# A hybrid decoder step on one core: the feed-forward's down projection as seven block products instead of eight, for 18 of its 22 feature tiles

## The chip, the cores and the metric

The kernel runs on one core of a Trainium2 chip. TensorE (PE) multiplies matrices into PSUM, VectorE (DVE), ScalarE (ACT) and GpSimd (POOL) work on tiles of 128 partitions, and SyncE (SP) and ACT issue transfers between DRAM and on-chip memory. The engines run side by side and wait for each other by semaphores. The metric is the device time of one execution in microseconds.

## The reference, cut to what matters

One layer of a decoder trunk for 1024 prompt tokens and 8 x 4 sample tokens (1056 columns in all): a mixer block, cross-attention, a feed-forward block and the final norm. The change touches the feed-forward block alone:

```python
u = rmsnorm(h, W['norm_ffn'][l])
h = h + (jax.nn.silu(u @ W['w_ffn_gate'][l]) * (u @ W['w_ffn_up'][l])) @ W['w_ffn_down'][l]
...
y = rmsnorm(h, W['norm_final'])
```

The model width is 1024 (8 tiles of 128), the hidden width 2816 (22 feature tiles of 128). All values are float32.

## The kernel before

*Precision.* Every large product is made of three matmuls: an operand is split into a rounded part (hi, by ACT) and the rest (lo, by DVE or POOL), and hi x hi, lo x hi and hi x lo are summed in PSUM.

*Layout.* Features lie on the partitions and the 1056 tokens along the free axis. For block products the tokens are halved (`TH` = 528 columns), and each half is cut in two again for PE (`HB` = 264 columns, index c).

*Gate and up.* The loop `for f in range(NF2)` takes feature tiles two at a time (11 pairs f), first a gate phase, then an up phase. Each phase multiplies a 2 x 2 block of weights by a 2 x 2 block of activations with seven block products instead of eight (`PRODUCTS`, `strassen`). The right-hand blocks (B11, B21, B22 and the sums T1 to T4 of the activations) are made once, ahead of the loop, in `sides`, and stay in 28 slots of the pool `sl`. The left-hand blocks are made on the way by `lefts`: for each pair of weight tiles POOL makes two sums (s1, s3), DVE two (s2, s4), then ACT and DVE split the seven blocks; `ahead_of` keeps that work two weight pairs ahead.

The block products land in PSUM tiles `st` (three buffers for four sums G[0] to G[3]). After product i the callback `gate` or `up` moves sums out of PSUM. Its first step (i = 0) is a copy of G[0] by ACT; the third product (i = 2) adds into the same G[0], so PE may begin it only after the copy. In the gate phase the results get SiLU; in the up phase they are multiplied into the four quarters s11, s12, s21, s22 of the pair's gated result (two by POOL, two by DVE; s12 comes last). Then four transfers on ACT's queue store the quarters in `hid_dram`. The quarters live in a ring of five tiles (`slot2`, `temps`).

*Down.* After the loop the 22 hidden tiles are read back (`load_hidden`), split, and multiplied by the down weights in four groups of 6, 6, 6 and 4 tiles (`FGROUPS`): for each of the 8 output tiles, and for three chunks of 352 columns, PE makes 6 x 3 matmuls (`unit`, L151 to L153), and DVE adds the PSUM tile to the residual h (L1414), which was kept in `h_dram`. In the fourth group the output is finished in three stretches of columns (`LAST`): sum, squares for the final norm, scaling, store.

*Order.* The instructions of PE and SP stand in the order of the code; those of ACT, DVE and POOL are put in order by a scheduler when the kernel is built. Every engine works through its own row of instructions.

Of the kernel before, what the change touches and what calls it, by code (L numbers as in the profile page):

```python
# [15 lines left out]
P = 128  # L16
# [4 lines left out]
NCH = 3  # L21
# [4 lines left out]
FT = FF // P  # L26
FGROUPS = ((0, 6), (6, 6), (12, 6), (18, 4))
LAST = ((0, 384), (384, 768), (768, T))
# [29 lines left out]
def hybrid_step(ctx, tc, xT, memT, consts_d, masks_d, wbd_d, poolw_d, spool_d, w_kv, w_xbc, w_dt, w_lg, w_pool, w_z, h0_d,  # L58
# [173 lines left out]
    h_dram = dr.tile([P, 8, T], F32, name="h_dram")  # L232
    hid_dram = dr.tile([P, FT, T], F32, name="hid_dram")

# [1001 lines left out]
    def lefts(pairs):  # L1236

        raws = []

        def load(i):  # L1240
            r = [fp.tile([P, DM], F32, tag="ar", name=nm("ar"), bufs=4, padded_shape=[P, T]) for _ in range(2)]
            for k in range(2):
                for t, src in zip(r, pairs[i]):
                    nc.sync.dma_start(t[:, k * 512:k * 512 + 512], src[:, k * 512:k * 512 + 512])
            raws.append(r)

        load(0)
        for i in range(len(pairs)):
            (a11, a12), (a21, a22) = [(t[:, :512], t[:, 512:]) for t in raws.pop(0)]
# [3 lines left out]
            s1, s2, s3, s4 = sa[:, :512], sa[:, 512:], sb[:, :512], sb[:, 512:]  # L1253
            nc.gpsimd.tensor_tensor(s1, a21, a22, op=OP.add)
            nc.gpsimd.tensor_tensor(s3, a11, a21, op=OP.subtract)
            nc.vector.tensor_tensor(s2, s1, a11, op=OP.subtract)
            nc.vector.tensor_tensor(s4, a12, s2, op=OP.subtract)
            for n, srcs in enumerate(((a11, s2), (a12, s3), (s1, a22), (s4,))):
                pool, b = (fp, "b") if n % 2 else (wp, "")
                hi, lo = (pool.tile([P, DM], F32R, tag=b + t, name=nm(t), bufs=2) for t in ("whi", "wlo"))  # L1260
                for j, src in enumerate(srcs):
                    a = slice(j * 512, j * 512 + 512)
                    nc.scalar.activation(hi[:, a], src, AF.Copy)  # L1263
                    nc.vector.tensor_tensor(lo[:, a], src, hi[:, a].bitcast(F32), op=OP.subtract)  # L1264
                yield [(hi[:, j * 512:j * 512 + 512], lo[:, j * 512:j * 512 + 512]) for j in range(len(srcs))]

# [13 lines left out]
    NF2 = FT // 2  # L1280
    blocks = ahead_of(lefts([(w_gu[j, 2 * f], w_gu[j, 2 * f + 1]) for f in range(NF2) for j in range(2)]))

    def product(i, w, G, c, kk):
        xb, g, begins = PRODUCTS[i]
        whi, wlo = w
        for k in range(kk):
            a, b = k * P, k * P + P
            xh, xl = X[xb, k, c]
            out = G[g][:, c, :HB]
# [4 lines left out]

    def strassen(kk, after, by_part):

# [12 lines left out]
        for i in range(7):  # L1309
            g = PRODUCTS[i][1]  # L1310
            if g not in G:
                G[g] = ps.tile([P, 2, 512], F32, tag="st", name=nm("st"), bufs=3)
            w = next(blocks)
            for c in range(2):
                product(i, w, G, c, kk)
            after(i, slice(0, 2), G)

    def temps():
        t = slot2(F32, "tm")
        return [t[:, i * TH:(i + 1) * TH].rearrange("p (c t) -> p c t", c=2) for i in range(2)]  # L1320

    add, sub, mul = OP.add, OP.subtract, OP.mult
    for f in range(NF2):
# [28 lines left out]
        v22, v12 = temps()  # L1352
        v21, _ = temps()

        def up(i, cs, G):
# [17 lines left out]
            else:  # L1373
                vec(u2, u2, at(2), op=add)
                vec(s12[:, cs], s12[:, cs], u2, op=mul)

        strassen(4, up, f == NF2 - 1)
        for n, t in enumerate(ga):
            nc.scalar.dma_start(hid_dram[:, 2 * f + n // 2, n % 2 * TH:(n % 2 + 1) * TH], t.rearrange("p c t -> p (c t)"))
    drain()  # L1380
    fp_.close()
# [6 lines left out]
    with tc.tile_pool(name="fq", bufs=1, reuse_waits="tile") as fp:  # L1388
        hids = []

        def load_hidden():
            f = len(hids)
            hi, lo = slot(F32R, "hh"), slot(F32R, "hl")
            nc.sync.dma_start(lo.bitcast(F32), hid_dram[:, f, :])
            nc.scalar.activation(hi, lo.bitcast(F32), AF.Copy)
            nc.vector.tensor_tensor(lo, lo.bitcast(F32), hi.bitcast(F32), op=OP.subtract)
            hids.append((hi, lo))

        weights = one_ahead([(w_down[m, :, f0 * P:(f0 + nf) * P], nf * P) for f0, nf in FGROUPS[:-1] for m in range(8)])
        for _ in range(FGROUPS[0][1]):  # L1400
            load_hidden()
        h = [slot2(F32, "h") if m < 5 else slot(name="h") for m in range(8)]
        nc.sync.dma_start(h[0], h_dram[:, 0, :])
        for f0, nf in FGROUPS[:-1]:
            for m in range(8):
                w = next(weights)
                if f0 == 0 and m < 7:
                    nc.sync.dma_start(h[m + 1], h_dram[:, m + 1, :])
                if len(hids) < min(f0 + nf + 6, FT):
                    load_hidden()  # L1410
                for c in range(NCH):
                    p = mmps()
                    unit(p, w, hids[f0:f0 + nf], ch(c), nf)
                    nc.vector.tensor_tensor(h[m][:, ch(c)], h[m][:, ch(c)], p, op=OP.add)  # L1414
        f0, nf = FGROUPS[-1]
        hid = hids[f0:]
        ws = []

        def last_strip():
            t = slot(F32R, "wd")  # L1420
            m = len(ws)
            split_into(w_down[m, :, f0 * P:(f0 + nf) * P], nf * P, t[:, :nf * P], t[:, nf * P:2 * nf * P])
            ws.append((t[:, :nf * P], t[:, nf * P:2 * nf * P]))

        while len(ws) < 8:
            last_strip()

        def finish(a, b, sq, n0, n1):
# [25 lines left out]
        for a, b in LAST:  # L1454
            for m in range(8):
                p = ps.tile([P, b - a], F32, tag="mm", name=nm("mm"), bufs=3)
                unit(p, ws[m], hid, slice(a, b), nf)
                hc = h[m][:, a:b]
                nc.vector.tensor_tensor(hc, hc, p, op=OP.add)
                sq = fp.tile([P, b - a], F32, tag="sq", name=nm("sq"), bufs=3, padded_shape=[P, 384])  # L1460
                if m:
# [6 lines left out]
            spawn(finish(a, b, sq, *((3, 3) if b < T else (0, 0))))  # L1468
        drain()
    ps_.close()  # L1470

# [4 lines left out]
def _layout(i):  # L1476
# [66 lines left out]
    a["w_gu"] = np.stack([strips(i["w_ffn_gate"][0]), strips(i["w_ffn_up"][0])])  # L1543
    a["w_down"] = strips(i["w_ffn_down"][0])
    return a
# [36 lines left out]
```

## Time and profile before

| | |
|---|---|
| time, median of 3 runs | 1827.39 us (1826.93 to 1829.48) |
| profiled execution | 1827.24 us, span 1825.3 us, mean granted clock 0.986 |
| gate and up phases | from 1073.5 us to 1546.2 us of the span |
| a pair f (gate and up) in steady state | 41.0 us |
| down, first 18 feature tiles | to 1760.5 us |
| down, last 4 tiles, and final norm | to 1825.3 us |

The page of the profile gives busy times; "granted clock" is the share of full speed that PE's clock had. A row of a timeline has start, duration, engine, line of the code, operation, and what it writes and reads (by the program's names, with shapes), and in brackets how long the engine stood idle before it and what ended that. "ACTq" is a transfer issued by ACT. In `st<-x,whi`, st is a PSUM tile, x a right-hand block and whi a left-hand block.

### The profile page before, as it was taken

Reading aid. Unit: us, or ns where it says so; the run is one execution under the profiler, and the core shown is the slowest. Engines: PE = TensorE matmul, PEld = TensorE weight load, DVE = VectorE, ACT = ScalarE, POOL = GpSimd, SP = SyncE. Lnnn points to the kernel's source line nnn. Section 1 sums busy time; section 2 is a strip of 40 time slices with the busy share of each in tenths; the row PEclk is TensorE's granted clock in tenths of the full one; section 3 lists DMA queues with packets and bytes.
Section 4 is the critical chain, followed back from the end, with each engine's and each line's share of the span. In section 5 each row is a group of like instructions: output and inputs, shape, how many; then the busy total and the mean of one; then the engine's idle time right before and its main releaser. Section 6 shows DMA issues by size and latency. Waiting matters only on the chain.

```text
span 1825.3 us, 30861 instructions
## 1 busy us (share of the span) xinstructions
PE 1747.0 (96%) x12043; PEld 1694.2 (93%) x12043; DVE 1091.0 (60%) x2043; ACT 743.5 (41%) x1445; POOL 533.2 (29%) x584
## 2 busy tenths in 40 slices
PE   8899999999999999999999879999999999999997
PEld 7798888888999999999999768999999999999997
DVE  5888997798744434455565587555555555443335
ACT  6544443577634213355564453322322223211134
POOL 2423557664342222212220332222222221000014
PEclk9999999999999999999999978999999999999999
DMA  9111123341322512144352132222222223532212
GB/s 347 56 61 61 62 63 90 103 143 56 128 82 74 191 60 94 66 144 128 116 181 96 34 129 87 78 71 76 86 72 77 77 73 132 195 98 93 80 50 96
DMA packets 96130, 182.84 MB, mean 100 GB/s; under 512 B 14192, under 2 KB 29168, under 8 KB 95984
## 3 DMA queue, kind: packets, MB, share of 16 engines
q1 hardware_dynamic: 78128, 147.04, 24.6%
q10 hardware_dynamic: 17856, 33.83, 5.0%
q8 instruction: 94, 1.54, 0.3%
q14 instruction: 52, 0.43, 0.1%
HBM read 144.24 MB, written 36.59 MB: 99 GB/s over the span
## 4 chain that ended last, share of the span: by engine, by line
PE 79%; DVE 10%; issue 3%; POOL 3%; ACT 2%; DMA 2%; SPq 0%; ACTq 0%; DVEq 0%; POOLq 0%
PE mm L151 15%; PE mm L153 15%; PE mm L152 15%; PE st L1291 8%; PE st L1292 8%; PE st L1290 8%; DVE cy L502 2%; PE poa L1081 1%; PE pss L1063 1%; DVE x L329 1%; POOL seg L574 1%; PE poz L1012 1%; DVE x L1179 1%; PE psa L1012 1%; DVE seg L557 1%
## 5 line engine op out<-in xcount | busy, mean ns | idle before, releaser
L1290 PE MATMUL st<-x,whi 128*128 128x264 f32 x1232 | 353.3, 287 | 7.7 <-DVE tm L1341 6.1
L1291 PE MATMUL st<-x,whi 128*128 128x264 f32 x1232 | 352.7, 286 | 3.1 <-DVE x L1179 3.1
L1292 PE MATMUL st<-x,wlo 128*128 128x264 f32 x1232 | 353.0, 287 | 0.5 <-DVE wlo L1264 0.5
L151 PE MATMUL mm<-uh,whi 128*128 128x352 f32 x960 | 319.9, 333 | 0.0
L153 PE MATMUL mm<-uh,wlo 128*128 128x352 f32 x960 | 310.5, 323 | 0.0
L152 PE MATMUL mm<-ul,whi 128*128 128x352 f32 x960 | 310.2, 323 | 0.0
L1290 PEld LDWEIGHTS st<-x,whi 128*128 128x128 f32 x1232 | 234.3, 190 | 8.8 <-DVE tm L1341 6.3
L1291 PEld LDWEIGHTS st<-x,whi 128*128 128x128 f32 x1232 | 233.8, 190 | 3.6 <-DVE x L1179 3.6
L1292 PEld LDWEIGHTS st<-x,wlo 128*128 128x128 f32 x1232 | 234.2, 190 | 0.9 <-DVE wlo L1264 0.9
L151 PEld LDWEIGHTS mm<-uh,whi 128*128 128x128 f32 x960 | 181.1, 189 | 4.3 <-issue 1.9
L152 PEld LDWEIGHTS mm<-ul,whi 128*128 128x128 f32 x960 | 181.6, 189 | 2.5
L153 PEld LDWEIGHTS mm<-uh,wlo 128*128 128x128 f32 x960 | 181.0, 189 | 0.0
L121 ACT ACTIVATE whi<-wraw 128x512 fp32r<-128x512 f32 (+1 forms) x176 | 100.3, 596 | 176.1 <-PE mm L152 143.6
L151 PE MATMUL mm<-hh,whi 128*128 128x352 f32 x432 | 140.3, 325 | 3.0 <-ACT whi L121 3.0
L153 PE MATMUL mm<-hh,wlo 128*128 128x352 f32 x432 | 140.2, 324 | 0.8 <-DVE wlo L122 0.8
L152 PE MATMUL mm<-hl,whi 128*128 128x352 f32 x432 | 139.9, 324 | 0.0
L122 DVE TENSOR_TENSOR wlo<-wraw,whi 128x512 fp32r<-128x512 f32 (+1 forms) x144 | 100.2, 721 | 23.3 <-ACT whi L121 22.9
L1414 DVE TENSOR_TENSOR h<-h,mm 128x352 f32<-128x352 f32 x72 | 37.4, 520 | 106.4 <-PE mm L153 106.4
L1263 ACT ACTIVATE whi<-as 128x512 fp32r<-128x512 f32 x88 | 54.8, 624 | 93.5 <-PE st L1291 74.6
L956 POOL TENSOR_TENSOR kvlo<-kvraw,kvhi 128x512 fp32r<-128x512 f32 x32 | 41.4, 1295 | 162.6 <-ACT kvhi L955 124.4
L1464 POOL TENSOR_TENSOR acc_mem<-acc_mem,sq 128x384 f32<-128x384 f32 (+1 forms) x18 | 17.6, 978 | 240.7 <-ACT sq L1462 240.2
L151 PEld LDWEIGHTS mm<-hh,whi 128*128 128x128 f32 x432 | 81.6, 189 | 3.3 <-ACT whi L121 3.3
(444 smaller groups left out, 4097.4 us busy)
## 6 DMA issues: line engine op xcount, KB each, us to landing
ar<-w_gu SPq DMA_DIRECT2D x88, 256.0 KB, 3.7
hid_dram<-tm ACTq DMA_DIRECT2D x44, 264.0 KB, 2.1
hl<-hid_dram SPq DMA_DIRECT2D x22, 528.0 KB, 4.1
h_dram<-h ACTq DMA_DIRECT2D x16, 528.0 KB, 2.9
h<-h_dram SPq DMA_DIRECT2D x16, 528.0 KB, 5.2
seg<-acs_dram SPq DMA_DIRECT2D x32, 256.0 KB, 3.6
wraw<-w_out SPq DMA_DIRECT2D x32, 256.0 KB, 3.6
kvraw<-kc_d SPq DMA_DIRECT2D x32, 256.0 KB, 2.9
```

The lines of the kernel that those rows point to most:

```text
L121: nc.scalar.activation(hi[:, a:b], raw, AF.Copy)
L122: (second if a else nc.vector).tensor_tensor(lo[:, a:b], raw, hi[:, a:b].bitcast(F32), op=OP.subtract)
L151: nc.tensor.matmul(out, whi[:, a:b], xh[:, cols], start=k == 0, stop=False)
L152: nc.tensor.matmul(out, whi[:, a:b], xl[:, cols], start=False, stop=False)
L153: nc.tensor.matmul(out, wlo[:, a:b], xh[:, cols], start=False, stop=k == kk - 1)
L502: nc.vector.scalar_tensor_tensor(y[:, :n], raw[:, j:j + n], w[j], y[:, :n], op0=OP.mult, op1=OP.add)
L956: eng.tensor_tensor(lo, src, hi.bitcast(F32), op=OP.subtract)
L1263: nc.scalar.activation(hi[:, a], src, AF.Copy)
L1290: nc.tensor.matmul(out, whi[:, a:b], xh, start=begins and k == 0, stop=False, skip_group_check=True)
L1291: nc.tensor.matmul(out, whi[:, a:b], xl, start=False, stop=False, skip_group_check=True)
L1292: nc.tensor.matmul(out, wlo[:, a:b], xh, start=False, stop=k == kk - 1, skip_group_check=True)
L1414: nc.vector.tensor_tensor(h[m][:, ch(c)], h[m][:, ch(c)], p, op=OP.add)
```

## The change

The down products of the first 18 feature tiles (9 pairs) become seven block products as well, in three groups of three pairs; the last four tiles stay as they were.

- The right-hand blocks are now quarters of the gated result and four sums of them. At the end of each of the first nine pairs f, POOL makes T1 to T4 from the quarters, and ACT's queue stores seven tiles of 528 columns (s11, s21, s22, T1 to T4) in place of four.
- `load_right` reads such a block back, ACT rounds it, and DVE (every third time POOL) makes the rest. Each group needs 21 of them (7 products x 3 pairs), each in one of the 28 slots; `feed` loads them as slots come free, in the last up phase and in the fourth block (m = 3) of each group.
- The down weights go through `lefts` too, in pairs of output tiles (width 384 instead of 512), and `down` adds the block products into h: three additions on POOL, six operations on DVE, one copy on ACT for each pair of output tiles.
- One PSUM pool serves gate, up and down; the change to the pool of the last stage comes after the down groups. The first loads of the down stage are issued in the second half of the last up phase.

The core of the diff:

```diff
-FGROUPS = ((0, 6), (6, 6), (12, 6), (18, 4))
+NG, GK = 3, 3
+F0 = NG * GK * 2
+NB8 = ("B11", "B12", "B21", "B22", "T1", "T2", "T3", "T4")
...
-    hid_dram = dr.tile([P, FT, T], F32, name="hid_dram")
+    hid_dram = dr.tile([P, FT // 2, 8, TH], F32, name="hid_dram")
...
+    def load_right():
+        b, f = next(rights)
+        t = slot(F32R, "xd")
+        hi, lo = t[:, :TH], t[:, TH:]
+        nc.sync.dma_start(lo.bitcast(F32), hid_dram[:, f, NB8.index(b)])
+        nc.scalar.activation(hi, lo.bitcast(F32), AF.Copy)
+        (nc.gpsimd if len(hids) % 3 == 2 else nc.vector).tensor_tensor(lo, lo.bitcast(F32), hi.bitcast(F32), op=OP.subtract)
+        hids.append(t)
+        for c in range(2):
+            X[b, 4 + f, c] = hi[:, c * HB:(c + 1) * HB], lo[:, c * HB:(c + 1) * HB]
...
+            if f == NF2 - 1 and cs.start == 0 and i == 6:
+                feed(12)
+                load_h(0)
+                load_h(1)
+            elif f == NF2 - 1 and cs.start == 1:
+                feed({0: 2, 4: 4, 5: 3}.get(i, 0))
 
         strassen(4, up, f == NF2 - 1)
-        for n, t in enumerate(ga):
-            nc.scalar.dma_start(hid_dram[:, 2 * f + n // 2, n % 2 * TH:(n % 2 + 1) * TH], t.rearrange("p c t -> p (c t)"))
+        if f < NG * GK:
+            t1, t3, t2, t4 = v22, v12, v21, v11
+            for t, x, y in ((t1, s12, s11), (t2, s22, t1), (t3, s22, s12), (t4, s21, t2)):
+                nc.gpsimd.tensor_tensor(t, x, y, op=sub)
+            parts = zip((0, 2, 3, 4, 5, 6, 7), (s11, s21, s22, t1, t2, t3, t4))
+        else:
+            parts = enumerate(ga)
+        for n, t in parts:
+            nc.scalar.dma_start(hid_dram[:, f, n], t.rearrange("p c t -> p (c t)"))
...
+    for g in range(NG):
+        for m in range(4):
...
+            def down(i, cs, G):
+                at = lambda g: G[g][:, cs, :HB]
+                vec, gp = nc.vector.tensor_tensor, nc.gpsimd.tensor_tensor
+                if i == 0:
+                    nc.scalar.activation(u3, at(0), AF.Copy)
+                elif i == 1:
+                    vec(u2, u3, at(1), op=add)
+                    gp(h12, h12, u2, op=add)
+                elif i == 2:
+                    vec(h11, h11, at(0), op=add)
+                elif i == 3:
+                    vec(u3, u3, at(1), op=add)
+                    gp(h22, h22, u3, op=add)
+                    gp(h21, h21, u3, op=add)
...
+                if m == 3:
+                    feed(3)
+
+            strassen(GK, down, k0=4 + g * GK)
```

How the rows of ACT change where one pair f ends and the next begins (here the sixth and the seventh). First before: the last two of the four stores of the quarters (tm_14053 and tm_14054 hold them), weight splits (whi), then the copy of the next pair's first product (tm_14493<-st):

```order
L1379 DMA hid_dram<-tm_14054 128x528
L1263 ACTIVATE whi_14553<-as_14393 128x512
L1379 DMA hid_dram<-tm_14053 128x528
L1333 ACTIVATE tm_14493<-st_14495 128x528
L1263 ACTIVATE whi_14620<-ar_14386 128x512
```

Now, at the same place (tm_14306 and tm_14307 hold the four sums):

```order
L1446 DMA hid_dram<-tm_14089 128x528
L1266 ACTIVATE whi_14595<-as_14428 128x512
L1446 DMA hid_dram<-tm_14306 128x528 x2
L1446 DMA hid_dram<-tm_14307 128x528 x2
L1387 ACTIVATE tm_14535<-st_14537 128x528
L1266 ACTIVATE whi_14662<-ar_14421 128x512
```

One store, of a quarter, stood ahead of the copy (L1333); four, of the sums, stand ahead of it now (L1387).

POOL at the same place, before: the two gated quarters, then two sums of the weights of the next pair:

```order
L1369 TENSOR_TENSOR tm_14053<-tm_14053,tm_14271 128x528
L1372 TENSOR_TENSOR tm_14054<-tm_14054,tm_14272 128x528
L1254 TENSOR_TENSOR as_14614<-ar_14387 128x512
L1255 TENSOR_TENSOR as_14615<-ar_14386,ar_14387 128x512
L1254 TENSOR_TENSOR as_14832<-ar_14609 128x512
```

And now:

```order
L1423 TENSOR_TENSOR tm_14088<-tm_14088,tm_14306 128x528
L1426 TENSOR_TENSOR tm_14089<-tm_14089,tm_14307 128x528
L1257 TENSOR_TENSOR as_14656<-ar_14422 128x512
L1258 TENSOR_TENSOR as_14657<-ar_14421,ar_14422 128x512
L1441 TENSOR_TENSOR tm_14306<-tm_14088,tm_14089 128x528
L1441 TENSOR_TENSOR tm_14306<-tm_14088 128x528
L1441 TENSOR_TENSOR tm_14307<-tm_14088,tm_14306 128x528
L1441 TENSOR_TENSOR tm_14307<-tm_14089,tm_14307 128x528
L1257 TENSOR_TENSOR as_14874<-ar_14651 128x512
```

The four sums (L1441) stand behind the weight sums (L1257, L1258), and the second and the fourth read the one before.

ACT where the second down group ends and the third begins, a place that before had no like (xd are right-hand blocks, whi weight splits, hh the first whole hidden tile for the last stage, tm<-st the copy of the third group's first product):

```order
L1266 ACTIVATE whi_18548<-ar_18328 128x384
L1337 ACTIVATE xd_18401<-xd_18401 128x528
L1337 ACTIVATE xd_18405<-xd_18405 128x528
L1266 ACTIVATE whi_18548<-as_18542 128x384
L1337 ACTIVATE xd_18434<-xd_18434 128x528
L1353 ACTIVATE hh_18438<-hl_18439 128x1056
L1465 ACTIVATE tm_18443<-st_18444 128x528
```

The copy stands last, behind the group's right-hand blocks and the hidden tile.

More of the change, by code (lines that the diff above doesn't have):

```diff
@@ L1280, in hybrid_step, with product @@
     NF2 = FT // 2
-    blocks = ahead_of(lefts([(w_gu[j, 2 * f], w_gu[j, 2 * f + 1]) for f in range(NF2) for j in range(2)]))
-    def product(i, w, G, c, kk):
+    GW = 2 * GK * P
+    blocks = ahead_of(lefts([(w_gu[j, 2 * f], w_gu[j, 2 * f + 1], 512) for f in range(NF2) for j in range(2)] +
+                            [(w_down[2 * m, :, g * GW:(g + 1) * GW], w_down[2 * m + 1, :, g * GW:(g + 1) * GW], GK * P)
+                             for g in range(NG) for m in range(4)]))
+    def product(i, w, G, c, kk, k0=0):
         xb, g, begins = PRODUCTS[i]
@@ L1293, in product, with strassen @@
         tick()
-    def strassen(kk, after, by_part):
+    def strassen(kk, after, by_part=False, k0=0):
         G = {}
@@ L1320, in temps, with load_h, load_hidden, last_strip @@
         return [t[:, i * TH:(i + 1) * TH].rearrange("p (c t) -> p c t", c=2) for i in range(2)]
+    rights = iter([(f"{PRODUCTS[i][0]}", g * GK + k) for g in range(NG) for i in range(7) for k in range(GK)])
+    hids = []
+    def load_right():
[8 more added lines that the diff above has]
+            X[b, 4 + f, c] = hi[:, c * HB:(c + 1) * HB], lo[:, c * HB:(c + 1) * HB]
+    def load_h(m):
+        h[m] = slot(name="h") if m < 3 else slot2(F32, "h")
+        nc.sync.dma_start(h[m], h_dram[:, m, :])
+    hid, ws = [], []
+    def load_hidden():
+        f = F0 + len(hid)
+        hi, lo = slot(F32R, "hh"), slot(F32R, "hl")
+        nc.sync.dma_start(lo.bitcast(F32), hid_dram[:, f // 2, f % 2 * 2:f % 2 * 2 + 2].rearrange("p s t -> p (s t)"))
+        nc.scalar.activation(hi, lo.bitcast(F32), AF.Copy)
+        nc.vector.tensor_tensor(lo, lo.bitcast(F32), hi.bitcast(F32), op=OP.subtract)
+        hid.append((hi, lo))
+    def last_strip():
+        t = slot(F32R, "wd")
+        m, nf = len(ws), FT - F0
+        split_into(w_down[m, :, F0 * P:], nf * P, t[:, :nf * P], t[:, nf * P:2 * nf * P])
+        ws.append((t[:, :nf * P], t[:, nf * P:2 * nf * P]))
+    tail = [load_hidden] * 4 + [last_strip] * 8
+    room = [0]
+    def feed(n):
+        room[0] += n
+        while len(hids) < 7 * NG * GK and room[0] >= 1:
+            load_right()
+            room[0] -= 1
+        while len(hids) == 7 * NG * GK and tail and room[0] >= (2 if tail[0] is load_hidden else 1):
+            room[0] -= 2 if tail[0] is load_hidden else 1
+            tail.pop(0)()
     add, sub, mul = OP.add, OP.subtract, OP.mult
@@ L1380, in hybrid_step @@
+    while tail:
+        tail.pop(0)()
     drain()
-    fp_.close()
     ps_.close()
@@ L1387, in hybrid_step @@
     ps = ps_.enter_context(tc.tile_pool(name="ps3", bufs=4, space=PSUM, reuse_waits="tile"))
[L1388 to L1426, printed above, removed]
+    if True:
         def finish(a, b, sq, n0, n1):
@@ L1543, in _layout @@
     a["w_gu"] = np.stack([strips(i["w_ffn_gate"][0]), strips(i["w_ffn_up"][0])])
-    a["w_down"] = strips(i["w_ffn_down"][0])
+    at = [2 * GK * g + 2 * k + j for g in range(NG) for j in range(2) for k in range(GK)] + list(range(F0, FT))
+    a["w_down"] = c(strips(i["w_ffn_down"][0]).reshape(8, P, FT, P)[:, :, at]).reshape(8, P, FF)
     return a
```

41 lines of the change are left out of this document (29 added, 12 removed).

## The prediction

> **What bounds the kernel now.** I read the page's busy shares and its chain first, then the windows of the feed-forward stages, then the timeline at one boundary between two pairs of feature tiles.
>
> ```profile
> span 1825.3 us, 30861 instructions
> PE 1747.0 (96%) x12043; PEld 1694.2 (93%) x12043; DVE 1091.0 (60%) x2043; ACT 743.5 (41%) x1445; POOL 533.2 (29%) x584
> PE 79%; DVE 10%; issue 3%; POOL 3%; ACT 2%; DMA 2%; SPq 0%; ACTq 0%; DVEq 0%; POOLq 0%
> ```
>
> PE is nearly full, and the chain runs through it. What the change touches lies after 1073 us, so the windows there give the price of a matmul (columns: stretch, its length, then busy time and number of instructions by engine, granted clock, DMA share, GB/s):
>
> ```profile
> 1200.00:1400.00 200.00, 200.00 (x1642) 200.00 (x1641) 103.84 (x145) 56.47 (x97) 47.02 (x29) 1.00 0.24 78
> 1546.50:1560.00 13.50, 9.93 (x50) 9.64 (x51) 7.22 (x11) 4.98 (x7) 0.00 (x0) 0.87 0.83 294
> 1560.00:1612.00 52.00, 52.00 (x325) 52.00 (x324) 20.89 (x35) 10.74 (x17) 0.00 (x0) 1.00 0.43 140
> ```
>
> The block products (264 columns) come every 200/1642 = 0.1218 us, the down matmuls (352 columns) every 52/325 = 0.160 us, and in both PE waits for nothing. A whole block of the gate or up phase is 168 matmuls, 20.5 us; one of its seven products is 24, 2.92 us. So matmuls saved are time saved, and any wait put before PE is time lost. The entry to the down stage is the one place there where PE waits:
>
> ```profile
> 1545.94 0.28 PE L1292 MATMUL st<-x,wlo 128*128 128x264 f32 x1
> 1549.27 0.43 PE L151 MATMUL mm<-hh,whi 128*128 128x352 f32 x1 [3.05 <-ACT whi L121]
> 1550.66 0.50 PE L153 MATMUL mm<-hh,wlo 128*128 128x352 f32 x1 [0.80 <-DVE wlo L122]
> 1550.96 0.49 PE L151 MATMUL mm<-hh,whi 128*128 128x352 f32 x1
> L151 PE MATMUL mm<-hh,wd x96: 290/337/442, 1760.5 to 1813.0; 128*128 128x384 f32 x64, 128*128 128x288 f32 x32
> ```
>
> From 1546.06 to 1760.5 the 18 tiles take 214.4 us.
>
> **The change, part by part.**
>
> *Products.* Before: 3 groups x 8 output tiles x 3 chunks x 6 tiles x 3 matmuls = 1296, at 0.160 us 207.4 us. After: 3 groups x 4 pairs x 7 products x 2 halves x 3 tiles x 3 = 1512 narrower ones, at 0.1218 us 184.2 us. That is -23.2 us. The other 214.4 - 207.4 = 7.0 us is the old entry (its gaps, and matmuls at half rate after them); it goes: -7.0 us. What is late there next comes below.
>
> *The four sums at each pair's end.* This term decides. The end of one pair and the start of the next, before, on all engines (start, duration, engine, line):
>
> ```profile
> 1344.45 0.70 DVE L1375 TENSOR_TENSOR tm<-tm,tm 128x528 f32<-128x528 f32 x1
> 1344.67 1.63 POOL L1255 TENSOR_TENSOR as<-ar,ar 128x512 f32<-128x512 f32 x1 [2.08 <-issue]
> 1345.07 1.78 DVE L1257 TENSOR_TENSOR as<-ar,as 128x512 f32<-128x512 f32 x1
> 1345.19 0.33 ACTq L1379 DMA_DIRECT2D hid_dram<-tm  x1
> 1345.61 0.61 ACT L1333 ACTIVATE tm<-st 128x528 f32<-128x528 f32 x1 [3.63 <-DMA ar<-w_gu]
> 1346.87 0.28 PE L1292 MATMUL st<-x,wlo 128*128 128x264 f32 x1
> 1346.99 0.28 PE L1290 MATMUL st<-x,whi 128*128 128x264 f32 x1
> ```
>
> DVE finishes the last gated quarter at 1345.15. ACT issues its transfer at 1345.19, as soon as that is done, and only then (1345.61) runs the copy of the next pair's first product out of PSUM, though that product ended near 1344.3. ACT works in order: the copy waits behind a transfer that waits. The copy ends at 1346.22; at 1346.99 PE begins the third product (24 matmuls after 1344.07), which adds into the bank just copied. So PE has 0.77 us to spare.
>
> Changed, the copy stands behind four more transfers, one for each sum, and POOL makes the sums after the quarter and after its row of L1255 (same work, ends 1346.30). Their price is from POOL's own 528-wide products of two tiles (a group's mean in 1300 to 1500 us; then one overlapped with DVE):
>
> ```profile
> L1369 POOL TENSOR_TENSOR tm<-tm,tm 128x528 f32<-128x528 f32 x4 | 5.3, 1323 | 45.9 <-DVE tm L1368 45.9
> L1372 POOL TENSOR_TENSOR tm<-tm,tm 128x528 f32<-128x528 f32 x4 | 6.8, 1705 | 6.4 <-DVE tm L1371 6.4
> 1339.63 1.81 DVE L1264 TENSOR_TENSOR wlo<-ar,whi 128x512 fp32r<-128x512 f32 x1
> 1339.19 1.70 POOL L1372 TENSOR_TENSOR tm<-tm,tm 128x528 f32<-128x528 f32 x1 [1.61 <-DVE tm L1371]
> ```
>
> Two-input work of DVE and POOL at once stretches both: 1.70 us on POOL for 1.32, 1.81 on DVE for 0.68. The first sum meets the rest of DVE's L1257, so 1.70; behind that DVE waits for ACT's copy, so the other three take 1.32: the last ends at 1351.97. Issue and gap as before (1345.61 - 1345.19 = 0.42) and the copy (0.61) bring 1353.0. PE waits 1353.0 - 1346.99 = 6.0 us. After a wait of that length the clock is slow:
>
> ```profile
> 1093.63 0.59 PE L1290 MATMUL st<-x,whi 128*128 128x264 f32 x1 [6.07 <-DVE tm L1341]
> 1094.02 0.42 PE L1291 MATMUL st<-x,whi 128*128 128x264 f32 x1
> 1094.24 0.42 PE L1292 MATMUL st<-x,wlo 128*128 128x264 f32 x1
> 1096.88 0.30 PE L1292 MATMUL st<-x,wlo 128*128 128x264 f32 x1
> 1097.03 0.28 PE L1290 MATMUL st<-x,whi 128*128 128x264 f32 x1
> ```
>
> Fifteen matmuls from 1093.63 took 3.40 us in place of 15 x 0.1218 = 1.83: 1.6 us more. So 7.6 us at each of the nine pairs that make sums: +68 us. Behind the waiting transfers on ACT are the copy, whose readers are DVE's first sum of products and PE, and two weight splits; those have a lead of five products and cost nothing. Bounds: four sums at 1.32 us and a full clock 5.6 x 9 = 50; four at 1.70 with the slow clock 8.7 x 9 = 78. I take 68, as both its rows are of this form and length.
>
> *Three more stores a pair* (264 KB) are nine times 0.8 MB where the DMA share is 0.24 (first window); hidden, and with no other cover needed.
>
> *The down stage's new waits.* Each group needs 21 right-hand blocks of half a hidden tile, loaded only as the group before frees its slots in its fourth block. A block is now 126 matmuls, 15.3 us, a product 2.19 us. The nearest rows are the whole tiles, of twice the width (landing; ACT; DVE; and what the transfers reached):
>
> ```profile
> hl<-hid_dram SPq DMA_DIRECT2D x22, 528.0 KB, 4.1
> L1395 ACT ACTIVATE hh<-hl x22: 1070/1087/1089, 1530.0 to 1713.9; 128x1056 fp32r<-128x1056 f32 x22
> L1396 DVE TENSOR_TENSOR hl<-hl,hh x22: 1250/1258/1259, 1531.1 to 1715.1; 128x1056 fp32r<-128x1056 f32 x22
> 1554.00:1558.00 4.00, 4.00 (x26) 4.00 (x25) 1.28 (x2) 1.09 (x1) 0.00 (x0) 0.96 1.04 410
> ```
>
> In the next group's first block ACT's copy stands behind 18 of the 21 splits; in the third group behind all, and behind a whole hidden tile of the tail. PE wants that copy at 15.3 + 2 x 2.19 = 19.7 us after the fourth block began. The last slots are free at 13.1 us (product 6), or 15.3 for the tail's tile. With 4.1 us to land, halves of 1.09 us to split (0.54 each, three) and 0.61 for the copy this is 19.4 us for the second group; for the third, 15.3 + 4.1 + 1.09 + 0.61 = 21.1. Twenty-one blocks and a weight pair are 6.5 MB, 15.9 us at 410 GB/s, beginning at 2.2: no slack either. I take 5 us at each of the two, slow clock included. At the entry the splits begin inside the last up phase, and ACT's first copy stands behind all 21 and a weight split that waits for PE's second product: 6 us. The change of PSUM pools moves to the tail: 1 us. Together +17 us. Bounds: 0, if all lands early, and 35, if each of the three is 8.4 us behind (the second rival) and the slow clock follows each (3 x 1.6) with the rest as it is (about 5).
>
> **Sum.** The profiled execution took 1827.24 us (span 1825.3 and 1.9 around it), the median is 1827.39. 1827.24 - 23.2 - 7.0 + 68 + 17 = 1882.0; 0.15 more for the median: 1882 us, 3.0% slower.
>
> **Rivals.**
>
> *Faster: the waiting transfers don't hold ACT's copy.* If a store that waits let the copy pass, the nine stalls would vanish: 1827.4 - 30.2 + 17 = 1814 us. It decides from the last sum's transfer being issued by 1345.9 in the rows above. Against it: 1345.19 and 1345.61, and the copy's 3.63 us of idle time with its product long done. Chance 0.06.
>
> *The shared work of POOL and DVE sets the down stage.* Around a group's change 14 splits on DVE (half of 1.258, 8.8 us) and 7 on POOL (1.32, 9.2 us) are added to two blocks, each of which already has on POOL three sums at 1.32 and two 384 wide of about 1.0 (5.9 us) and on DVE nine operations 384 wide of about 0.5 us (0.68 at 512; 4.6 us). Laid end to end that is 39 us in 30.7: 8.4 us behind at each change, 25 at three, in place of 16: 1891 us, and with the slow clock after each 1896. The rows at 1339 us show the two engines stretching each other, though not fully: POOL's operation had begun first and was lengthened all the same. The Trainium skill ("SBUF — State Buffer", section "SBUF: two separate sides") calls that port pair an exclusive lock, held for a whole instruction while the other blocks. By that rule the operations do lie end to end and the time is this rival's; POOL's 1.70 for 1.32 says that the one that came first is slowed too, so the trace agrees with the sum of both more than with the lock. Chance 0.17.
>
> *The clock stays up.* Without the half-rate stretch: 9 x 6.0 = 54, 1868 us. Against it stand both gaps quoted (6.07 us, and 3.05 us followed by matmuls 0.30 us apart where 0.160 is normal). Chance 0.10.
>
> *Half hidden.* If POOL begins the sums as soon as the quarter is there (1345.2) and runs them at half the price, PE waits some 2 us and keeps its clock: 9 x 2 = 18, 1832 us. No row of POOL has such a price (0.66 us for 528). Chance 0.07.
>
> **How the numbers follow.** My forecast 0.60, the rivals 0.06, 0.17, 0.10, 0.07. The forecast's own range is 1864 (50 for 68) to 1900 (78 for 68 and 8 more in the down stage). The range asked reaches down to 1855, with the clock rival and an undisturbed down stage, and up to 1905, with the port rival and dearer sums; it leaves out the faster and the half-hidden rival and a little above. What a measurement can tell from no change is 0.2%, 3.7 us: faster 0.06, same 0.02, slower 0.92.
>
> **What the profile after would show.** At nine places 41 us and a wait apart, a PE idle of about 6 us before the third product of a gate phase, released by ACT's copy, which itself stands right behind four hid_dram stores, and a granted clock below 1 behind each; POOL rows of about 1.32 us on the sums' line, the first of each four longer. In the down stage 264-wide matmuls 0.122 us apart, and waits only in the first block of a group. The forecast is wrong if PE's rows at the third product show no idle time, or if the down stage, from the last up matmul to the first of the last four tiles, isn't near 201 us.

## The result, and the profile after

The changed kernel took 1911.8 us (median of 4 runs, 1907.1 to 1913.9) against 1828.4 us for the kernel before, run beside it (4 runs, 1826.9 to 1829.7): a ratio of 1.0453, with a 95% interval of 1.0429 to 1.0476. That is 4.5% slower. The forecast was 1882 us with a range from 1855 to 1905: the sign was right, the loss was 83 us where 55 were expected, and the time lies above the range. The profiled run took 1910.1 us, its span is 1908.3.

First the page's totals of the changed kernel (span, then busy time by engine):

```profile
span 1908.3 us, 31899 instructions
PE 1754.3 (92%) x12259; PEld 1698.2 (89%) x12259; DVE 1176.0 (62%) x2127; ACT 782.3 (41%) x1538; POOL 705.5 (37%) x701
```

PE's share fell from 96 to 92%. Where it fell is read from three rows of PE's groups: the third matmul of the gate and up products (its first and last start bound the feed-forward stage) of the kernel before,

```profile
L1292 PE MATMUL st<-x,wlo x1232: 279/285/422, 1074.0 to 1545.9; 128*128 128x264 f32 x176
```

the same of the kernel after, and its first product of the last four feature tiles, which ends the down stage:

```profile
L1298 PE MATMUL st<-x,wlo x1232: 279/285/422, 1075.0 to 1621.2; 128*128 128x264 f32 x176
L153 PE MATMUL mm<-hh,wd x96: 288/337/443, 1843.2 to 1896.3; 128*128 128x384 f32 x64, 128*128 128x288 f32 x32
```

The feed-forward stage grew from 471.9 to 546.2 us, +74.3. The down stage (1621.2 to 1843.2) takes 222.0 us, and took 214.6: +7.4, where 201 had been forecast. What follows took 65.1 us after and 64.8 before. The waits of PE in the kernel after (engine, line, releaser; total, count, longest):

```profile
PE st L1296 <- ACT tm L1387: 52.4, 9, 5.8
PE st L1296 <- DVE h L1476: 13.9, 2, 7.1
PE st L1296 <- ACT tm L1465: 12.1, 3, 6.1
```

The first row is the nine gate phases. One boundary between two pairs, all engines but PE, then PE itself:

```profile
1385.96 1.78 DVE L1260 TENSOR_TENSOR as<-ar,as 128x512 f32<-128x512 f32 x1
1387.15 1.75 POOL L1441 TENSOR_TENSOR tm<-tm,tm 128x528 f32<-128x528 f32 x1
1388.86 1.29 POOL L1441 TENSOR_TENSOR tm<-tm 128x528 f32<-128x528 f32 x1
1388.93 4.21 ACTq L1446 DMA_DIRECT2D hid_dram<-tm  x4
1390.12 2.66 POOL L1441 TENSOR_TENSOR tm<-tm,tm 128x528 f32<-128x528 f32 x2
1393.18 0.61 ACT L1387 ACTIVATE tm<-st 128x528 f32<-128x528 f32 x1 [10.31 <-POOL tm L1441]
```

```profile
1387.76 0.28 PE L1298 MATMUL st<-x,wlo 128*128 128x264 f32 x1
1393.85 0.59 PE L1296 MATMUL st<-x,whi 128*128 128x264 f32 x1 [5.80 <-ACT tm L1387]
1394.23 0.42 PE L1297 MATMUL st<-x,whi 128*128 128x264 f32 x1
...
1396.43 0.42 PE L1298 MATMUL st<-x,wlo 128*128 128x264 f32 x1
...
1396.83 0.28 PE L1297 MATMUL st<-x,whi 128*128 128x264 f32 x1
```

Read from the bottom up: PE starts its third product at 1393.85 because ACT's copy ended; the copy began at 1393.18 because the last of four stores had been issued; the stores were issued one by one as POOL's sums ended, from 1388.93 on. Then PE runs at half rate (a matmul every 0.22 us) until 1396.65.

The second row of the waits was not in the forecast. Around the first change of group, DVE and POOL stand so:

```profile
1687.14 0.69 DVE L1472 TENSOR_TENSOR tm<-tm,st 128x528 f32<-128x528 f32 x1
1687.76 0.69 DVE L1338 TENSOR_TENSOR xd<-xd 128x528 fp32r<-128x528 f32 x1
1687.91 1.70 POOL L1473 TENSOR_TENSOR h<-h,tm 128x528 f32<-128x528 f32 x1 [1.88 <-PE st L1298]
1688.38 1.65 DVE L1267 TENSOR_TENSOR wlo<-ar,whi 128x384 fp32r<-128x384 f32 x1
...
1689.58 1.61 POOL L1474 TENSOR_TENSOR h<-h,tm 128x528 f32<-128x528 f32 x1
1689.95 1.65 DVE L1267 TENSOR_TENSOR wlo<-as,whi 128x384 fp32r<-128x384 f32 x1
1691.15 3.32 POOL L1338 TENSOR_TENSOR xd<-xd 128x528 fp32r<-128x528 f32 x2
1691.52 3.51 DVE L1338 TENSOR_TENSOR xd<-xd 128x528 fp32r<-128x528 f32 x2
1694.96 0.69 DVE L1476 TENSOR_TENSOR h<-h,st 128x528 f32<-128x528 f32 x1
```

L1476 takes product 5's result out of PSUM; product 7 adds into the same bank, 2.19 us after product 5 ends. It stands in DVE's row behind two weight splits of 1.65 us and two block splits of 1.75 us each, and DVE is never idle: PE waited until 1695.71 (7.11 us). This is in the fourth block of the group, where the next group's blocks are loaded, not in the first block of the next group.

### The profile page after: what moved, and what is told of

It is laid out like the page before. It is cut to its first block, busy times and chain, and to the rows that moved or that the text cites. A ratio compares the mean times of both kernels' runs of the same rounds, so it can differ in the third digit from the quotient of the medians.

```text
span 1908.3 us, 31899 instructions
## 1 busy us (share of the span) xinstructions
PE 1754.3 (92%) x12259; PEld 1698.2 (89%) x12259; DVE 1176.0 (62%) x2127; ACT 782.3 (41%) x1538; POOL 705.5 (37%) x701
## 5 line engine op out<-in xcount | busy, mean ns | idle before, releaser
L1296 PE MATMUL st<-x,whi 128*128 128x264 f32 x1232 | 363.6, 295 | 62.7 <-ACT tm L1387 52.4
L1297 PE MATMUL st<-x,whi 128*128 128x264 f32 x1232 | 360.5, 293 | 3.0 <-DVE x L1181 3.0
L1296 PEld LDWEIGHTS st<-x,whi 128*128 128x128 f32 x1232 | 243.0, 197 | 66.4 <-ACT tm L1387 54.3
L1297 PEld LDWEIGHTS st<-x,whi 128*128 128x128 f32 x1232 | 242.4, 197 | 3.5 <-DVE x L1181 3.5
L1296 PE MATMUL st<-xd,whi 128*128 128x264 f32 x504 | 148.9, 295 | 26.0 <-DVE h L1476 13.9
L1297 PE MATMUL st<-xd,whi 128*128 128x264 f32 x504 | 148.1, 294 | 0.0
L1298 PE MATMUL st<-xd,wlo 128*128 128x264 f32 x504 | 147.7, 293 | 0.0
L1266 ACT ACTIVATE whi<-as 128x512 fp32r<-128x512 f32 (+1 forms) x136 | 79.6, 586 | 155.1 <-PE st L1297 105.8
L1296 PEld LDWEIGHTS st<-xd,whi 128*128 128x128 f32 x504 | 100.0, 198 | 27.0 <-DVE h L1476 14.3
L1257 POOL TENSOR_TENSOR as<-ar 128x512 f32<-128x512 f32 (+1 forms) x34 | 51.1, 1503 | 193.8 <-DVE wlo L1267 185.2
L1266 ACT ACTIVATE whi<-ar 128x512 fp32r<-128x512 f32 (+1 forms) x102 | 59.9, 587 | 150.0 <-PE st L1297 125.0
L123 ACT ACTIVATE whi<-wraw 128x512 fp32r<-128x512 f32 x128 | 77.9, 626 | 106.0 <-PE mm L154 76.0
L1267 DVE TENSOR_TENSOR wlo<-as,whi 128x512 fp32r<-128x512 f32 (+1 forms) x136 | 111.1, 818 | 0.1
```

Source lines behind the costliest of these rows:

```text
L123: nc.scalar.activation(hi[:, a:b], raw, AF.Copy)
L1296: nc.tensor.matmul(out, whi[:, a:b], xh, start=begins and k == 0, stop=False, skip_group_check=True)
L1297: nc.tensor.matmul(out, whi[:, a:b], xl, start=False, stop=False, skip_group_check=True)
L1298: nc.tensor.matmul(out, wlo[:, a:b], xh, start=False, stop=k == kk - 1, skip_group_check=True)
```

## The experiments

All stages below are read as above: the feed-forward stage between the first and the last start of the third gate and up matmul, the down stage from there to the first matmul of the last four tiles. What lies before the feed-forward stage moved its start between 1069.7 and 1079.6 us from run to run, so the stages say more than the totals of single runs. Times of single runs unless said; the kernel before, run beside each of them, took 1826.1 to 1827.7 us.

| kernel | time us | feed-forward us | down us |
|---|---|---|---|
| before (profiled) | 1827.2 | 471.9 | 214.6 |
| after (profiled) | 1910.1 | 546.2 | 222.0 |
| sums' stores on SyncE's queue | 1840.95 | 474.6 | 223.3 |
| three of four stores late | 1872.36 | 506.3 | 223.5 |
| sums on DVE | 1833.88 | 477.1 | 220.7 |
| POOL's splits left out | 1901.08 | 545.2 | 212.4 |
| splits on DVE | 1901.03 | 547.0 | 213.8 |
| splits and additions on DVE | 1897.94 | 549.0 | 200.6 |
| no reload | 1880.78 | 546.7 | 189.9 |
| sums, splits, additions on DVE | 1827.48 | 479.3 | 204.0 |
| the same, reload over two blocks | 1823.92 | 478.9 | 202.3 |
| the same, entry too | 1815.58 | 476.3 | 198.4 |
| the same, evacuation first (5 runs) | 1811.63 | 475.8 | 194.4 |
| that order, POOL keeps splits and additions | 1824.34 | 478.3 | 204.9 |

**The nine stalls: which queue, and how many sums.** Three kernels change only how the sums are made or how they reach DRAM. In the first the four stores go to SyncE's queue, in the middle of the next gate phase.

```diff
+            while later:                       # in the next gate phase, after i == 5
+                fl, n, t = later.pop(0)
+                nc.sync.dma_start(hid_dram[:, fl, n], ...)
...
-            nc.scalar.dma_start(hid_dram[:, f, n], ...)
+            if n < 4: nc.scalar.dma_start(hid_dram[:, f, n], ...)
+            else:     later.append((f, n, t))
```

> POOL still makes the four sums, but their four stores are issued from SyncE's queue in the middle of the next pair's gate phase, so ACT's copy of the next pair's first product has no waiting store of a sum ahead of it. Theory W (the copy waits in ACT's row behind stores that wait for POOL): the nine PE waits of 5.8 us and the half-rate stretch of about 2.1 us behind each go, 9 x 7.9 = 71 us, so the feed-forward stage falls from 547 to about 476 us and the time to about 1841 us. Theory S (the sums themselves are the price, by POOL and DVE stretching each other or by late buffers): PE keeps waiting for most of that, and the time stays above 1890 us. The down stage is untouched and should keep its 222 us in either case.

Measured: 1840.95 us, the feed-forward stage 474.6, 71.6 us shorter, and no wait of PE for the copy between 1110 and 1540 us. POOL still makes all 36 sums there. So the sums themselves are not the price; their stores, ahead of the copy in ACT's row, are.

The second kernel keeps `nc.scalar` in the same place; in its order one store of a sum stands ahead of the copy and three behind.

> The same four stores stay on ACT's queue but are written later; one store of a sum still stands ahead of the copy, three behind it. Theory W: the wait scales with the number of sums that the copy stands behind, so one sum (about 1.75 us, the stretched first one) leaves a PE wait of 5.8 - 2.66 - 1.3 = about 1.8 us at each of nine pairs, with little or no half-rate stretch: some 52 us less than after, about 1858 us. Theory S: 1890 us or more.

Measured: 1872.36 us; PE's waits are now

```profile
PE st L1296 <- ACT tm L1388: 18.0, 9, 2.0
```

Four sums ahead of the copy: 5.8 us; one: 2.0 (1.8 expected); none: 0. But the stage lies 31.7 us above the one without waits, 3.5 us a pair and not 2.0: the time is 14 us worse than expected. Most of the rest is the clock. Ten microseconds from two of the nine waits of this kernel (PE's matmuls in brackets, then the other engines, granted clock, DMA share, GB/s):

```profile
1280.80:1290.80 10.00, 10.00 (x70) 10.00 (x71) 3.81 (x6) 2.92 (x5) 2.64 (x3) 0.84 0.26 97
1325.50:1335.50 10.00, 10.00 (x82) 10.00 (x83) 4.57 (x7) 3.00 (x6) 2.71 (x3) 1.00 0.36 125
1368.80:1378.80 10.00, 10.00 (x70) 10.00 (x71) 3.81 (x6) 2.92 (x5) 2.66 (x3) 0.83 0.26 98
```

In seven of nine the clock is 0.83 or 0.84 and 12 or 13 matmuls are lost, 12 x 0.1218 = 1.5 us; in two it stays at 1.00. In the kernel after, the same stretch has three values:

```profile
1148.50:1158.50 10.00, 10.00 (x60) 10.00 (x61) 3.00 (x5) 2.68 (x5) 0.00 (x0) 0.70 0.05 18
1198.20:1208.20 10.00, 10.00 (x67) 10.00 (x68) 3.77 (x6) 2.73 (x5) 0.00 (x0) 0.80 0.06 20
1247.10:1257.10 10.00, 10.00 (x71) 10.00 (x72) 3.74 (x6) 2.69 (x5) 0.00 (x0) 0.86 0.07 23
```

60, 67 and 71 matmuls of 82 are 2.7, 1.8 and 1.3 us lost, on average 1.9; the other six waits are followed by 61, 67 or 68, and 71 matmuls, in the same order twice more. The Trainium skill ("TensorE: Matmul & The Clock Gate", Part 1, "The HAM clock gate") says that the gate looks at a free-running window of about 3.4 us, so that the slow stretch varies from run to run; the three values for waits of the same length (5.80 to 5.84 us) agree with that. It puts the throttled state after an idle window of that length; here 2.0 us of waiting were enough in seven cases of nine.

The third kernel changes the engine of the sums:

```diff
-                nc.gpsimd.tensor_tensor(t, x, y, op=sub)
+                nc.vector.tensor_tensor(t, x, y, op=sub)
```

> The four sums are made by DVE (about 0.7 us each) instead of POOL; the copy now stands ahead of the waiting stores, and DVE's first sum of products stands behind the four sums. Theory W: four times 0.7 us is shorter than what PE has to spare plus the copy, so PE waits at most 1 us at each pair and the time is 1840 to 1850 us. Theory S as a matter of POOL beside DVE would also give this; theory S as late buffers gives 1890 us or more. Together with the run that moves the stores this tells whether POOL's slowness or the queue matters: if only the queue matters, both runs give the same time within 5 us.

Measured: 1833.88 us, lower than expected, with no such wait left. A boundary of it (ACT's queue and rows, DVE's sums):

```profile
1299.88 0.61 ACT L1387 ACTIVATE tm<-st 128x528 f32<-128x528 f32 x1 [2.28 <-PE st L1298]
...
1302.39 0.69 DVE L1441 TENSOR_TENSOR tm<-tm,tm 128x528 f32<-128x528 f32 x1
...
1303.12 2.31 ACTq L1446 DMA_DIRECT2D hid_dram<-tm  x4
```

The copy now stands ahead of the four stores and waits for PE alone. The feed-forward stage is 2.5 us from that of the kernel with the stores on SyncE's queue, so either cure takes the nine stalls; the 7 us between the totals are mostly the start of the stage (1076.2 against 1069.7).

**The down stage: is it the loading at all?**

```diff
-        X[b, 4 + f, c] = hi[...], lo[...]
+        for g in range(NG): X[b, 4 + f + g * GK, c] = hi[...], lo[...]
...
-        while len(hids) < 7 * NG * GK and room[0] >= 1:
+        while len(hids) < 7 * GK and room[0] >= 1:
```

> Groups 2 and 3 multiply by group 1's right-hand blocks, so 42 of the 63 loads and splits of the down products are left out (the products of these groups are computed with other data); matmuls, weight sums, evacuations and the entry stay. Theory: all of the down stage above its 184 us of products is the price of loading right-hand blocks. The waits at the two changes of group (7.1 + 2.1 and 6.8 + 4.0 us) and the half-rate stretches behind them go, the entry's wait of 6.1 us and its stretch of about 2 us stay: down stage 184 + 8 to 10 = about 193 us in place of 222, time about 1883 us. Rival (the seven evacuations of a block, 2.19 us apart, are too dense for DVE and POOL without any loading): waits spread over all twelve blocks, and the time stays above 1900 us.

Measured: a down stage of 189.9 us, with one wait left (4.2 us, at the entry). 184.2 forecast for the products, 4.2 and about 1.5 of slow clock make that up: the product term was right. (The entry's wait was 6.1 us in the kernel after. The first two blocks of the second group, loaded there, are left out here as well; whether that shortens it was not followed up.) Of the rest, 222.0 - 189.9 = 32.1 us, the entry's shorter wait is 1.9; what is left is the two changes of group, about 15 us each, where the forecast had 5. POOL's additions to the hidden quarters are all still there: without the loading PE waits there for none of DVE's sums. The last stage grew by 4 us; PE waits 2.2 us there for a strip of the last tiles, which are loaded later in this kernel.

**The down stage: whose work is late?** Three kernels move or remove POOL's work.

```diff
-        (nc.gpsimd if len(hids) % 3 == 2 else nc.vector).tensor_tensor(lo, ...)
+        if len(hids) % 3 != 2: nc.vector.tensor_tensor(lo, ...)      # left out
+        nc.vector.tensor_tensor(lo, ...)                             # splits on DVE
...
-                vec, gp = nc.vector.tensor_tensor, nc.gpsimd.tensor_tensor
+                vec = gp = nc.vector.tensor_tensor                   # and additions
```

> Of the right-hand blocks of the down products, POOL's third of the splits is left out (their low halves stay unsplit copies of the block, so those products are computed with other data); DVE's and ACT's splits, the transfers and the matmuls stay. Theory P (DVE and POOL lengthen each other around a change of group, so DVE's sum into the hidden quarter ends late): the two PE waits of 6.8 to 7.1 us for that sum go, and so does the half-rate stretch behind each (about 2 us), DVE's 384-wide rows there fall from 1.65 to 0.6-0.9 us, and the down stage goes from 222 to about 203 us: about 1893 us. Theory L (blocks land late or ACT's copy is late, not the shared work): waits of the same length remain at these two places and the time stays at 1906 to 1912 us. The feed-forward stage keeps its nine waits in both.

Measured: a down stage of 212.4, not 203; the two waits went from 7.1 and 6.8 to 3.3 and 3.0 us. Half right: DVE still stands behind weight splits lengthened by POOL's additions to the hidden quarters.

> All splits of right-hand blocks go to DVE; POOL keeps the three additions to the hidden quarters of a block. In the run without POOL's splits, DVE's row between two evacuations still held 384-wide weight splits of 1.66 to 1.69 us (0.55 alone), next to POOL's additions, and PE's two waits fell from 7 to 3.3 us. Theory P (DVE and POOL lengthen each other, in sum of work): DVE takes seven more splits of 0.70 us a group, but is not lengthened by POOL's; the two waits come out between 3.3 us and 3.3 + 2 x 0.70 = 4.7 us, the down stage near 215 us, the time near 1904 us. Theory C (too much work on DVE by count, whoever runs beside it): the waits grow above 7 us and the time is at or above 1912 us.

Measured: a down stage of 213.8 us, the two waits 3.5 us each, as theory P had it, and a third of 2.2 us for the same line in the next group's first block. DVE does seven more splits a group and PE waits half as long as in the kernel after.

> Splits and the three additions to hidden quarters of each down block go to DVE; POOL keeps only the weight sums. Theory P: DVE's weight splits fall back to 0.55 us beside PE's products and the block's splits to 0.70 us, so although DVE has more to do its own row ends earlier, the two waits for L1476 (7.1 and 6.8 us) go or fall below 2 us, and the down stage is near 222 - 18 = 204 us: about 1894 us. Theory C: DVE, with some 5 us more of work at each change of group, is later and the waits grow: above 1912 us. ACT's three waits (6.1, 4.0, 2.1 us) stand in both.

Measured: 200.6 us, better than expected, though the two waits stay at 4.2 us, above the 2 expected; of ACT's three (6.1, 4.0, 2.1 us) only the entry's is left, 3.3 us. The mean of the 384-wide weight splits of DVE, kernel after and then this one, from 1620 to 1845 us (busy, mean ns):

```profile
L1267 DVE TENSOR_TENSOR wlo<-as,whi 128x384 fp32r<-128x384 f32 x46 | 49.2, 1069 | 0.0
```

```profile
L1267 DVE TENSOR_TENSOR wlo<-as,whi 128x384 fp32r<-128x384 f32 x48 | 27.6, 575 | 0.1
```

And the same 16 us of the first change, after and this kernel (columns as before; DVE is third):

```profile
1683.00:1699.00 16.00, 8.89 (x62) 8.68 (x61) 15.44 (x17) 6.11 (x12) 10.40 (x7) 0.83 0.78 271
```

```profile
1684.00:1700.00 16.00, 11.81 (x85) 11.60 (x84) 16.00 (x28) 12.70 (x24) 0.00 (x0) 0.89 0.93 324
```

DVE is full in both, but does 28 instructions where it did 17, while POOL's seven cost 10.4 us. So two things were there: POOL's work lengthens DVE's (theory P), and without it DVE's row is still full for these 16 us (theory C, for what is left).

**Both parts together, and what is left.** With the sums on DVE as well:

> The sums, the splits of right-hand blocks and the additions to the hidden quarters all go to DVE. The two parts of the loss lie in different stages, so they should add: the run with the sums on DVE gave 1833.9 us, of which the down stage was 220.6; with the down stage of the run above (204 us if theory P holds) the time is 1833.9 - 17 = about 1817 us, below the 1827 us of before. If theory C holds instead, it is above 1834 us.

Measured: 1827.48 us, the time of before and not 1817. The down stage is as expected (204.0). Of the 10 us too much, 5.9 lie ahead of the change: the feed-forward stage starts at 1075.6 us and not at 1069.7, as it did in the run that the sum was built on. The stage itself is 2.2 us longer (479.3; its last up phase waits 2.2 us for DVE, which has more splits there), and so is what follows the down stage.

Next, the loading is spread, since DVE is full only around the change:

```diff
                 if m == 3:
-                    feed(3)
+                    feed(3 if g == NG - 1 else 2)
+                elif m == 0 and g:
+                    feed({0: 2, 1: 2, 2: 1, 4: 2}.get(i, 0))
```

> As the run with sums, splits and additions on DVE, but the 21 blocks of the next group are loaded two a product in the fourth block (14) and the other seven in the first products of the next group's first block, instead of three a product. Theory N (what is left at a change of group, 4.2 us of waiting for L1476 and about 2 us of slow clock, is DVE's own row being overfull in the fourth block): with a third of the splits moved into the next block the two waits fall below 1.5 us and the time is 1827.5 - 10 to 12 = about 1816 us. Rival (the blocks moved later now land too late: each needs about 5.5 us from issue to its split, and the last product of the first block wants its own 13.1 us after the block's begin): new PE waits for xd or for ACT's splits appear in the first block of groups 2 and 3, and the time stays at 1825 to 1832 us.

Measured: 1823.92 us, 3.6 us less than the run before, where 10 to 12 were expected; the down stage is only 1.7 us shorter. The 4.2 us became 1.7 in the fourth block and 2.2 in the next one, again for L1476's line: part of the wait moved along with the splits. None is for a transfer or for ACT's splits, so the rival's cause did not show, but its size nearly did.

```diff
-                feed(12)                                  # last up phase, first half
+                feed(9)
-                feed({0: 2, 4: 4, 5: 3}.get(i, 0))
+                feed({0: 2, 4: 3, 5: 2}.get(i, 0))
...
-            if (g, m) == (0, 0): feed(2)
-                elif m == 0 and g:
+                elif m == 0:
```

> As the run before, and the same spreading at the entry: 16 blocks are loaded in the last up phase and seven in the first down block, instead of 21 and two. Theory N: the last up phase's waits (0.7 and 2.2 us) and the entry's (4.4 us) with their slow clock shrink by about half, 4 to 6 us less than the run before: about 1811 us. Rival (the entry is set by transfers, 300 to 390 GB/s there, not by the splits' place in the rows): no change within 2 us, or new waits inside the first down block.

Measured: 1815.58 us; the two stages together (674.7 against 681.2) are 6.5 us shorter, a little above the 4 to 6 expected. The entry's wait falls from 4.6 to 0.8 us, with a new one of 2.7 later in the block.

Last, the additions that nobody waits for are written behind the sums that free PSUM:

```diff
                 elif i == 3:
                     vec(u3, u3, at(1), op=add)
-                    gp(h22, h22, u3, op=add)
-                    gp(h21, h21, u3, op=add)
                 elif i == 4:
                     vec(h22, h22, at(2), op=add)
+                    gp(h22, h22, u3, op=add)
                 elif i == 5:
                     vec(h21, h21, at(3), op=add)
+                    gp(h21, h21, u3, op=add)
```

(and h12's, from product 2 to product 3, in the same way)

> As the run with the entry spread too, and of the work of each down product the sum that reads PSUM is written first: the additions of the copied product to the hidden quarters, which nobody waits for, come one product later, behind the PSUM readers. Theory N (what is left, six waits of 0.8 to 2.7 us for L1474 and ACT's copy, is the place of DVE's evacuation of product 5 in its row, behind two additions of 0.70 us and splits): each of the five waits for DVE loses 1.4 us and some of the slow clock, 7 to 10 us in all: about 1807 us, 1.1% below before. Rival (DVE is full in these blocks, so order doesn't matter): the waits move to another product, and the time stays within 3 us of 1815.6.

Measured in 5 rounds: 1811.6 us (1809.0 to 1814.1), a ratio to before of 0.9908 (0.9894 to 0.9923). The down stage is 4.0 us shorter than in the run before, of 7 to 10 expected. Its waits and the 16 us around its first change:

```profile
PE st L1296 <- DVE h L1472: 3.8, 4, 1.5
PE st L1296 <- DVE tm L1465: 2.6, 5, 1.1
```

```profile
1602.00:1618.00 16.00, 15.55 (x128) 15.33 (x127) 15.25 (x25) 10.16 (x20) 1.21 (x1) 1.00 0.93 318
```

PE does 128 matmuls in the 16 us and the clock stays at 1.00; DVE is as full as before, with the right instruction in front. Of the 10.2 us still above the products' 184.2, 6.4 are these waits and 1.2 two more, for ACT. This version beats both kernels.

> The same spreading and order of writing, with POOL keeping the additions to the hidden quarters and its third of the splits as in the changed kernel; the sums are on DVE. Against the run with sums on DVE alone (1833.9 us) this is the order alone, against the run beside it POOL's share alone. Theory P (POOL beside DVE lengthens DVE's rows, 0.55 to 1.65 us): waits of 3 to 5 us at each change of group remain and the time is 10 us or more above the run beside it, near 1820 us. Rival (order is all): within 4 us of the run beside it.

Measured: 1824.34 us, a down stage of 204.9. Against sums on DVE alone (220.7) the spreading of the loads and the order together are worth 15.8 us; how much of that is order alone, with POOL at work, no run shows (without POOL it was 4.0 us, the run before). Against the run beside it (194.4) POOL's share costs 10.5 us: PE waits 10.6 us for L1472's line in five places, at most 3.1, where 3.8 stood. Both halves of the story are there, of similar size. Its row at the same place:

```profile
1618.97 1.32 POOL L1473 TENSOR_TENSOR h<-h,tm 128x528 f32<-128x528 f32 x1 [2.81 <-DVE h L1472]
1619.43 1.28 DVE L1267 TENSOR_TENSOR wlo<-as,whi 128x384 fp32r<-128x384 f32 x1
1620.26 1.63 POOL L1476 TENSOR_TENSOR h<-h,tm 128x528 f32<-128x528 f32 x1
1620.63 1.67 DVE L1267 TENSOR_TENSOR wlo<-ar,whi 128x384 fp32r<-128x384 f32 x1
```

## Why the prediction was right in sign and too small

- *Products, -23.2, and the old entry, -7.0.* Right: without reloading, the down stage is 189.9 us with one wait in it, 184.2 plus 5.7.
- *The four sums, +68.* The mechanism was right, with its parts close: four POOL rows, the first longer (1.75, 1.70 forecast), the copy right behind the stores, a wait of 5.8 (6.0). The slow clock was under-sized: one row had given 1.6 us, nine stalls give 1.3 to 2.7. From the kernel without the waits to the kernel after it is 71.6 / 9 = 7.96 us a pair where 7.6 stood; with 2.3 us of waits in the last up phase, of which the forecast had none, the stage is +74.3. Inside the bounds given (50 to 78).
- *The down stage's new waits, +17, is the step that failed.* They are 222.0 - 184.2 = 37.8 us, above the upper bound of 35: 26.0 us of waits, and 11.8 behind them, nearly all of it slow clock (0.71 to 0.83 granted in the 10 us after each). The entry was right (6.1 us). At the two changes the forecast looked at ACT's copy in the next group's first block only (5 us each), and these waits came out as 2.1 and 4.0 us. It overlooked that in the fourth block, where the splits are made, DVE must also free PSUM within 2.19 us, from a row that the splits fill. Those two waits are 7.1 and 6.8 us, with the slow clock after them. DVE's splits were not on its path at all; there they take 1.75 us each.
- *The rival of POOL's and DVE's shared work* named that cause, with a chance of 0.17, and put the time at 1891 to 1896. It too was too small: it charged 8.4 us a change, 10 with the slow clock, and each change costs about 15. It counted each engine's work over two blocks, where the wait is decided by one instruction's place in one row within one product. The experiments support the rival's cause for a good part (10.5 us in the reordered kernel, 8 to 21 in the three that take work from POOL) and the place of DVE's work in its row, spread over blocks and with the PSUM sums first, for a part as large (15.8 us).
- *The rivals of a clock that stays up, a store that lets the copy pass, and a half-hidden sum* are out: 0.70 to 0.86 granted behind each stall, the copy 10.31 us idle behind the stores, and sums of 1.29 to 1.75 us.
- *The sum.* 1827.2 + 74.3 + 7.4 + 0.3 for the last stage + 1.0 for a later start = 1910.2, the profiled time. Against the forecast the feed-forward stage is 6 us dearer and the down stage 21.

## What to carry to other kernels

A store that waits for a slow producer, put on the queue of an engine that also has to free PSUM, costs PE the whole wait, less what PE has to spare, at each place. Moving the store to an idle queue, or making the sums on a faster engine, took that wait away here (about 70 us); the products saved came through only when the waits of the down stage were shortened too. When work is added to an engine that evacuates PSUM, don't add up its busy time over a stage: look for the instruction on which PE waits, count what stands ahead of it within one product, and write that instruction first. Where two engines take turns at their operands, as DVE and POOL do in the rows below, count their rows as one.

## What the runs showed of the hardware

- *DVE and POOL take turns.* The four rows of the last experiment, quoted above, fit one rule: an operation with two inputs outside PSUM waits until the other engine's is done, and the profile counts the waiting as its time. POOL's 1.32 us at 1618.97 is its undisturbed price (the forecast's group of POOL products has 1.32 too). DVE's split begins behind it at 1619.43 and ends at 1620.71, 0.42 us after POOL's (0.55 alone). POOL's next begins at 1620.26, ends at 1621.89, 1.18 us after DVE's, and counts 1.63; DVE's next counts 1.67 and ends 0.41 us behind that. The prediction read the POOL row of 1.70 at 1339.19 as one that came first and was slowed all the same. The row of DVE just before that pair was not looked at:

```profile
1339.03 0.68 DVE L1264 TENSOR_TENSOR wlo<-as,whi 128x512 fp32r<-128x512 f32 x1
```

This split runs until 1339.71, POOL's row ends 1.18 us behind it, as above, and DVE's 1.81 ends 0.55 us behind POOL's: nothing is stretched, each waits its turn. The Trainium skill ("SBUF — State Buffer", section "SBUF: two separate sides") speaks of an exclusive lock that the one which starts first keeps for its whole instruction. These rows agree with it, and the doubt that the prediction cast on it was wrong.
- *The sums that free PSUM are not lengthened.* In the kernel after, between 1640 and 1840 us, L1476 (one input in PSUM) takes 0.69 or 0.70 us in all twelve cases, ten of them begun while a row of POOL was running; the twenty splits `wlo<-as` begun beside POOL take 1.65 to 1.69 us where 0.55 is normal. What came late is the evacuation's start, by the splits ahead of it, and not the evacuation.
- *A wait of 2.0 us can be enough for the slow clock*: seven times in nine a granted clock of 0.83 or 0.84 over the next 10 us, 1.5 us lost on top of 2.0. It is not sure to come: behind the wait of 2.7 us of the version with the entry spread, and behind 3.3 us at the entry of the one with splits and additions on DVE, 82 matmuls ran in 10 us, at a granted clock of 1.00. In the version with the evacuation first, PE's waits at the same stages are at most 1.5 us and its longest 264-wide matmul of the down products is 0.40 us, so none ran in the stretches of 0.42 that follow the long waits.
